# Copying projections out of PSUM at once, and handing a tile's attention outputs over behind the next tile's scores

## The chip, the core and the metric

The kernel runs on one core of a Trainium2 chip. The metric is the device time of the program in microseconds (us). TensorE (PE) multiplies and writes to PSUM; VectorE (DVE), ScalarE (ACT) and GpSimd (POOL) compute; SyncE (SP) only issues DMAs. ACT and POOL can issue DMAs as well. Each engine works through its own instructions in order.

## The reference, cut to what matters

One layer is computed for a prompt of 1024 tokens (tiles 0 to 7 of 128 rows) and for 8 x 16 new sample tokens (tile 8):

```python
n1 = rmsnorm(h); qa, ka, va, fl, qb, kb, vb, ga, gb = split(n1 @ w_in)
qa, ka, qb, kb = rmsnorm per head           # 8 heads x 64 in each of two mixers
log_f = log_sigmoid(fl + b_f); c = cumsum(log_f)
ya = softmax(qa @ ka.T / 8 + c_i - c_j, causal) @ va            # mixer A
yb = softmax(qb @ kb.T / 8 + relative bias, band of 9 chunks of 64) @ vb   # mixer B
# the sample tokens attend to 2048 (A) or 512 (B) cached rows per sequence as well
h += (sigmoid(ga) * (ya @ w_up_a) + sigmoid(gb) * (yb @ w_up_b)) @ w_out
h += PEER(rmsnorm(h))     # 8 heads pick 16 of 16384 experts: two top-16 and a gather
h += sigmoid(rmsnorm(h) @ w_ple_gate) * (p @ w_ple_proj)
```

k, v and log_f of the new tokens are outputs too. Weights and activations of the large products are split into a high and a low part, and a product is made of three matmuls.

## The kernel before, in words

The tiles are in two groups: group 0 is tiles 8, 0, 1, 2, group 1 is tiles 3 to 7. The phases of the span follow each other: norm and attention of group 0 (to about 500 us), its merge (gates and w_out), routing of group 0 (its remainder reaches into the next stretch), attention of group 1 (790 to 1391 us), its merge, routing of group 1 (to about 2010 us), `expand_phase` (2010 to 2256 us), `dense_phase` (to about 3870 us) and `ple_phase`. The experts of group 0 are fetched by 1024 gathers (`gather_steps`, POOL issues, DVE multiplies and adds), which are laid between the other work from the attention of group 1 on: 400 of them before `expand_phase`, the others in `dense_phase`. Matmuls `hd` of 36 blocks of experts (`hidden_phase`) fill PE in routing and expansion.

The attention of a group walks over eight units (`UNITS`; a unit is two heads of one mixer: 0 to 3 of A, 4 to 7 of B). For each unit, `project` makes a tile's projection `z` (k, q, v in 384 columns, 24 matmuls) in one of two PSUM banks of pool `z`, normalises k and q into `kq`, copies v into `vU`, transposes k and q through a bank `tp` and keeps them as `kT` and `qp`. Between the projections of a unit stand the attention steps of the unit before (`last`): `prompt` for prompt tiles, `decode` for tile 8. `prompt` makes, for each of the two heads, the scores `N` in a PSUM bank, the row minimum on DVE, `softmax_rows` (two passes of ACT and a reciprocal on DVE) into `p`, transposes of `p` into a bank `pt`, their copies `pT` (L80, called from `evac`), and the output matmuls `po` (L497), which use 64 of the 128 columns of the array: head 0 writes partitions 0 to 63 of `po`, head 1 partitions 64 to 127. The banks `tp`, `pt`, `po` share one pool, with three banks for group 0 and two for group 1. `decode` does the same against the cached rows `kcd` and `vcd`, which SP loads into a ring of `KC` buffers; its output matmuls `pod` (L591) use 32 columns each, for four sequences in turn.

The order within an engine is not written by hand. A scheduler walks over the program with a priority that follows the order of the code (shifted for some phases: gathers, routing and `hidden_phase` come later than their place) and a model of when buffers are free, and it fixes each engine's list; a buffer that is asked for while all of its pool are held must be waited for. SP's loads and stores are one such list.

## Time and profile before

| | us |
|---|---|
| median of 3 runs | 4042.02 |
| lowest and highest run | 4021.49, 4048.87 |
| the profiled execution | 4036.04 |
| its span in the profile | 4033.9 |
| PE busy in the span | 3674.5 (91%) |
| DVE busy | 2939.1 (73%) |
| POOL busy | 1865.5 (46%) |
| ACT busy | 1446.2 (36%) |

The span is the time from the first to the last instruction of the program in one execution; 2.1 us of the execution lie around it. A busy share is an average over phases with different limits, and a busy PE can still be a PE that is behind. PEld is PE's loading of weights, which can lie beside matmuls.

### The profile page before, as it was taken

Reading aid. Unit: us, or ns where it says so; the run is one execution under the profiler, and the core shown is the slowest. Engines: PE = TensorE matmul, PEld = TensorE weight load, DVE = VectorE, ACT = ScalarE, POOL = GpSimd, SP = SyncE. Lnnn points to the kernel's source line nnn. Section 1 sums busy time; section 2 is a strip of 40 time slices with the busy share of each in tenths; the row PEclk is TensorE's granted clock in tenths of the full one; section 3 lists DMA queues with packets and bytes.
Section 4 is the critical chain, followed back from the end, with each engine's and each line's share of the span. In section 5 each row is a group of like instructions: output and inputs, shape, how many; then the busy total and the mean of one; then the engine's idle time right before and its main releaser. Section 6 shows DMA issues by size and latency. Waiting matters only on the chain.

```text
span 4033.9 us, 57386 instructions
## 1 busy us (share of the span) xinstructions
PE 3674.5 (91%) x20520; PEld 3032.9 (75%) x20520; DVE 2939.1 (73%) x5531; ACT 1446.2 (36%) x3307; POOL 1865.5 (46%) x1440
## 2 busy tenths in 40 slices
PE   7998899868888798899898899999999999999989
PEld 6555567656676565699898888888888888888866
DVE  5122202899887776889998698888888888888862
ACT  5444422346555510223488422222222222222231
POOL 5111032127667655553276355555555555555510
PEclk9999999879999999899999999999999999999999
DMA  6777733328888888983345789988989898989942
GB/s 207 239 237 208 229 96 120 103 74 262 276 284 263 285 317 297 329 268 115 109 189 219 274 307 310 320 311 310 330 313 317 307 325 314 325 302 307 313 159 72
DMA packets 415118, 1002.50 MB, mean 249 GB/s; under 512 B 38816, under 2 KB 170352, under 8 KB 412400
## 3 DMA queue, kind: packets, MB, share of 16 engines
q0 software_dynamic: 147456, 536.94, 38.7%
q1 hardware_dynamic: 267376, 461.90, 34.4%
q8 instruction: 161, 2.64, 0.3%
q14 instruction: 125, 1.02, 0.1%
HBM read 917.19 MB, written 81.50 MB: 248 GB/s over the span
## 4 chain that ended last, share of the span: by engine, by line
PE 30%; DVE 19%; DMA 19%; issue 18%; POOL 12%; ACT 2%; SPq 0%; POOLq 0%; DVEq 0%; ACTq 0%
DMA v<-in_pv,gi 7%; POOL u L813 6%; DMA u<-in_pu,gi 6%; PE hd L964 5%; POOL v L813 3%; DVE gya L818 3%; DVE u L816 3%; PE pg L933 3%; PE Sd L547 2%; PE py L1015 2%; PE py L1017 2%; PE py L1016 2%; PE pu L638 1%; DMA vs<-in_pv 1%; PE z L209 1%
## 5 line engine op out<-in xcount | busy, mean ns | idle before, releaser
L813 POOL DMA_INDIRECT v<-in_pv,gi x512 | 680.3, 1329 | 582.8 <-DVE gya L818 451.2
L813 POOL DMA_INDIRECT u<-in_pu,gi x512 | 663.4, 1296 | 505.7 <-DVE u L816 374.8
L816 DVE SCALAR_TENSOR_TENSOR u<-u,gn 128x1024 f32<-128x1024 f32 x512 | 628.2, 1236 | 169.0 <-DMA u<-in_pu,gi 167.3
L818 DVE SCALAR_TENSOR_TENSOR gya<-v,hid,gya 128x1024 f32<-128x1024 f32 x512 | 661.3, 1292 | 120.0 <-DMA v<-in_pv,gi 115.5
L1015 PE MATMUL py<-vh,wh 128*128 128x512 f32 x1280 | 507.7, 398 | 44.2 <-ACT wh L946 23.6
L964 PE MATMUL hd<-aTh,uh 128*128 128x320 f32 x2048 | 485.1, 314 | 24.0 <-ACT gp L967 13.7
L1017 PE MATMUL py<-vh,wl 128*128 128x512 f32 x1280 | 498.3, 395 | 5.8 <-DVE wl L947 5.5
L1016 PE MATMUL py<-vl,wh 128*128 128x512 f32 x1280 | 502.8, 394 | 0.0
L964 PE MATMUL hd<-aTh,ul 128*128 128x320 f32 x2048 | 484.1, 314 | 5.5 <-DVE ul L947 4.2
L964 PE MATMUL hd<-aTl,uh 128*128 128x320 f32 x2048 | 484.1, 313 | 0.0
L964 PEld LDWEIGHTS hd<-aTh,uh 128*128 128x128 f32 x2048 | 351.9, 191 | 35.1 <-ACT gp L967 15.0
L964 PEld LDWEIGHTS hd<-aTh,ul 128*128 128x128 f32 x2048 | 349.6, 190 | 12.6 <-DVE ul L947 6.9
L964 PEld LDWEIGHTS hd<-aTl,uh 128*128 128x128 f32 x2048 | 351.3, 191 | 4.0
L1015 PEld LDWEIGHTS py<-vh,wh 128*128 128x128 f32 x1280 | 242.9, 190 | 102.3 <-ACT wh L946 29.7
L946 ACT CAST vh<-vs 128x1024 fp32r<-128x1024 f32 x128 | 134.0, 1052 | 483.3 <-DMA vs<-in_pv 241.9
L1017 PEld LDWEIGHTS py<-vh,wl 128*128 128x128 f32 x1280 | 243.2, 190 | 61.2 <-DVE wl L947 10.6
L1016 PEld LDWEIGHTS py<-vl,wh 128*128 128x128 f32 x1280 | 242.9, 190 | 46.9
L946 ACT CAST uh<-us 128x1024 fp32r<-128x1024 f32 x128 | 134.2, 1048 | 293.0 <-PE hd L964 285.3
L946 ACT CAST wh<-ge 128x640 fp32r<-128x640 f32 x128 | 91.9, 727 | 402.7 <-DVE ge L993 213.4
L1018 DVE TENSOR_TENSOR yacc<-yacc,py 128x1024 f32<-128x1024 f32 x160 | 192.5, 1215 | 15.0 <-PE py L1017 15.0
L497 PE MATMUL po<-pT,vU 128*64 128x128 f32 x1056 | 153.0, 290 | 34.6 <-ACT pT L80 34.0
L933 PE MATMUL pg<-obb,ga 128*128 128x128 f32 x1280 | 158.8, 279 | 26.5 <-POOL ga L924 19.5
(1051 smaller groups left out, 7361.0 us busy)
## 6 DMA issues: line engine op xcount, KB each, us to landing
us<-in_uT SPq DMA_DIRECT2D x128, 512.0 KB
vs<-in_pv SPq DMA_DIRECT2D x128, 512.0 KB
G_d<-stage SPq DMA_DIRECT2D x10, 4096.0 KB
gj<-G_d SPq DMA_DIRECT2D x64, 640.0 KB
kcd<-in_kA SPq DMA_DIRECT2D x128, 256.0 KB
vcd<-in_vA SPq DMA_DIRECT2D x128, 256.0 KB
ge_d<-gp SPq DMA_DIRECT2D x36, 320.0 KB
ge<-ge_d SPq DMA_DIRECT2D x36, 320.0 KB
```

The source lines that it names most:

```text
L497: nc.tensor.matmul(po[64 * h:64 * h + 64, 0:P], vU[:, k0 + j, 64 * h:64 * h + 64], pT[:, j, :], start=j == 0, stop=j == nk - 1)
L547: nc.tensor.matmul(ps[32 * b4:32 * b4 + 32, :], q3[:, 4 * s + b4, :], rhs, start=br == 1 and q < nch, stop=True)
L813: nc.gpsimd.indirect_dma_start(out=r, out_offset=None, in_=I["pu" if k < P else "pv"], in_offset=bass.IndirectOffsetOnAxis(ap=gi[:, kk:kk ...
L816: nc.vector.scalar_tensor_tensor(r, r, 1.0, n2, op0=OP.mult, op1=OP.mult, accum_out=hid[:, kk:kk + 1])
L818: nc.vector.scalar_tensor_tensor(ya, r, hid[:, kk:kk + 1], ya, op0=OP.mult, op1=OP.add)
L933: nc.tensor.matmul(pg[:, c * P:(c + 1) * P], ga[:, b0 + c, :], ob[:, b0 + c, :], start=True, stop=True)
L946: nc.scalar.copy(out_h, src)
L964: nc.tensor.matmul(ps[sp][:, 0:Nw], a[:, k, :], b[:, k, sp * Nw:(sp + 1) * Nw], start=k == 0 and q == 0, stop=k == 7 and q == 2)
L1015: nc.tensor.matmul(py[:, c], wh[:, ns], vh[:, c], start=a, stop=False)
L1016: nc.tensor.matmul(py[:, c], wh[:, ns], vl[:, c], start=False, stop=False)
L1017: nc.tensor.matmul(py[:, c], wl[:, ns], vh[:, c], start=False, stop=z)
L1018: nc.vector.tensor_tensor(yacc[n], yacc[n], py, op=OP.add)
```

## The change

The change has six parts; the first four lie in the attention.

- `project` copies k and q (256 columns) and v out of the bank `z` by two ACT copies at once; the squares, and the multiplication by the norm, then read the copy in SBUF. Before, the squares and DVE's multiplication read `z`, and v was copied last.
- `prompt` ends after the softmax of both heads and gives back a function `outputs`, which makes the transposes, the copies `pT` and the output matmuls. `order` puts a tile's `outputs` behind the next tile's scores (the last tile's at the end of its unit). The bank `po` is asked for after the transposes and no longer at the start.
- The output matmuls take the two heads in turn: block j of head 0, block j of head 1, block j + 1 of head 0.
- The stores of k, v, log_f, of `kT_d` and `v_d`, and further on those of `ge_d` (`hidden_phase`) and `G_d` (`expand_phase`), are issued by ACT and no longer by SP: 215 in all, 160 of them in `project`.
- Buffers: `KC` 17 for 15, three `p` for two, one `Dn` for two, `qp` of group 0 six for eight. `sel_p` holds 8 columns and is broadcast to 128 where it is read (its making is left out of the diff, as are lines that only take the new `PB`).
- `expand_phase` makes each one-hot tile `oa` by two DVE instructions of 128x512, where it was one of 128x1024.

```diff
-KC = 15
+KC = 17
...
-PB = (2, 2)
+PB = ((3, 2), (3, 2))
...
-    sel_p = const.tile([P, 8, P], F32R, name="sel_p")
+    sel_p = const.tile([P, 8], F32R, name="sel_p")
...
-                Dn = at.tile([P, 2, 256], F32, tag="Dn", name=f"Dn{g}{u}")
+                Dn = at.tile([P, 2, 256], F32, tag="Dn", name=f"Dn{g}{u}", bufs=1)
...
+            vt = vU[:, slot[t], :]
+            nc.scalar.copy(kq, z[:, 0:256])
+            nc.scalar.copy(vt, z[:, 256:384])
+            sq = at.tile([P, 64], F32, tag="sq", name=f"sq{nm}", bufs=2)
             for h in range(4):
-                nc.scalar.activation(kq[:, 64 * h:64 * h + 64], z[:, 64 * h:64 * h + 64], AF.Square, accum_out=ss[:, h:h + 1])
+                nc.scalar.activation(sq, kq[:, 64 * h:64 * h + 64], AF.Square, accum_out=ss[:, h:h + 1])
             r = rstd_of(ss[:, 0:4], 64, 4, f"kq{nm}")
-            nc.vector.tensor_tensor(kq.rearrange("p (h c) -> p h c", h=4), z[:, 0:256].rearrange("p (h c) -> p h c", h=4),
-                                    r.unsqueeze(2).broadcast_to([P, 4, 64]), op=OP.mult)
+            k4 = kq.rearrange("p (h c) -> p h c", h=4)
+            nc.vector.tensor_tensor(k4, k4, r.unsqueeze(2).broadcast_to([P, 4, 64]), op=OP.mult)
             nc.vector.tensor_tensor(kq[:, 0:P], kq[:, 0:P], kn[:, br, :], op=OP.mult)
-            vt = vU[:, slot[t], :]
-            nc.scalar.copy(vt, z[:, 256:384])
...
             if ko is not None:
-                nc.sync.dma_start(ko[rows, cu * P:(cu + 1) * P], kq[:, 0:P])
-                nc.sync.dma_start(vo[rows, cu * P:(cu + 1) * P], vt)
+                nc.scalar.dma_start(vo[rows, cu * P:(cu + 1) * P], vt)
...
-            qp = at.tile([P, 2, P], F32, tag="qp", name=f"qp{nm}", bufs=2 * nts if g == 0 else nts + 1)
+            qp = at.tile([P, 2, P], F32, tag="qp", name=f"qp{nm}", bufs=nts + 2 if g == 0 else nts + 1)
...
                 nc.scalar.copy(kTs, tp[:, 0:P])
+                nc.scalar.dma_start(ko[rows, cu * P:(cu + 1) * P], kq[:, 0:P])
...
+                if ko is not None:
+                    nc.scalar.dma_start(ko[rows, cu * P:(cu + 1) * P], kq[:, 0:P])
...
-                    nc.sync.dma_start(kT_d[u, :, t * P:(t + 1) * P], kT[:, t * P:(t + 1) * P])
-                    nc.sync.dma_start(v_d[u, :, t, :], vt)
-                pending.append([lambda: prompt(g, u, br, t, n, qp, kT, vU, Dn, at, yT)])
+                    nc.scalar.dma_start(kT_d[u, :, t * P:(t + 1) * P], kT[:, t * P:(t + 1) * P])
+                    nc.scalar.dma_start(v_d[u, :, t, :], vt)
+                tail = []
+                pending.append([lambda: tail.append(prompt(g, u, br, t, n, qp, kT, vU, Dn, at, yT)), lambda: tail[0]()])
...
-            if TS not in tiles:
-                return p
-            d = p[tiles.index(TS)]
-            r = [x for i, x in enumerate(p) if i != tiles.index(TS)]
-            out = [[d[0]], [r[0][0], d[1]], [r[1][0], d[2]], [r[2][0], d[3]]]
+            d = [[f] for f in p[tiles.index(TS)]] if TS in tiles else [[] for _ in p]
+            r = [x for i, x in enumerate(p) if tiles[i] != TS]
+            k = len(d) - len(r)
+            out = d
+            for i, (scores, outputs) in enumerate(r):
+                out[i + k] = [scores] + out[i + k]
+                out[min(i + k + 1, len(out) - 1)].append(outputs)
             return out
...
-        po = bank(f"po{nm}")
+        ps_ = []
...
-                    nc.tensor.matmul(N[:, c0:c1], sel_p[:, 2 * u + h, :], cP[:, c0:c1], start=False, stop=not last)
+                    nc.tensor.matmul(N[:, c0:c1], sel_p[:, 2 * u + h:2 * u + h + 1].broadcast_to([P, P]), cP[:, c0:c1], start=False, stop=not last)
...
-            p = softmax_rows(N[:, 0:W], W, m, at, f"{nm}{h}")
-            pT = at.tile([P, pmax[0] // P, P], F32, tag="pT", name=f"pT{nm}{h}", bufs=PB[pmax[0] > 512])
-            for j0 in range(0, nk, 4):
-                j1 = min(nk, j0 + 4)
-                ps = bank(f"pt{nm}{h}{j0}")
-                for j in range(j0, j1):
-                    nc.tensor.transpose(ps[:, (j - j0) * P:(j - j0 + 1) * P], p[:, j * P:(j + 1) * P], ident)
-                evac(pT[:, j0:j1, :], ps[:, 0:(j1 - j0) * P].rearrange("p (j c) -> p j c", c=P))
+            ps_.append(softmax_rows(N[:, 0:W], W, m, at, f"{nm}{h}"))
+
+        def outputs():
+            pTs = []
+            for h, p in enumerate(ps_):
+                pT = at.tile([P, pmax[0] // P, P], F32, tag="pT", name=f"pT{nm}{h}", bufs=PB[pmax[0] > 512][1])
+                for j0 in range(0, nk, 4):
+                    j1 = min(nk, j0 + 4)
+                    ps = bank(f"pt{nm}{h}{j0}")
+                    for j in range(j0, j1):
+                        nc.tensor.transpose(ps[:, (j - j0) * P:(j - j0 + 1) * P], p[:, j * P:(j + 1) * P], ident)
+                    evac(pT[:, j0:j1, :], ps[:, 0:(j1 - j0) * P].rearrange("p (j c) -> p j c", c=P))
+                pTs.append(pT)
+            po = bank(f"po{nm}")
             for j in range(nk):
-                nc.tensor.matmul(po[64 * h:64 * h + 64, 0:P], vU[:, k0 + j, 64 * h:64 * h + 64], pT[:, j, :],
-                                 start=j == 0, stop=j == nk - 1)
-        nc.scalar.copy(yT[:, u, n * P:(n + 1) * P], po[:, 0:P])
+                for h, pT in enumerate(pTs):
+                    r = slice(64 * h, 64 * h + 64)
+                    nc.tensor.matmul(po[r, 0:P], vU[:, k0 + j, r], pT[:, j, :], start=j == 0, stop=j == nk - 1)
+            nc.scalar.copy(yT[:, u, n * P:(n + 1) * P], po[:, 0:P])
+
+        return outputs
...
-                nc.vector.tensor_tensor(oa, iota_i.unsqueeze(1).broadcast_to([P, 2, P, 4]),
-                                        rb[:, 0, cw].rearrange("p (b c) -> p b c", b=2).unsqueeze(2).broadcast_to([P, 2, P, 4]),
-                                        op=OP.is_equal)
+                for b in range(2):
+                    nc.vector.tensor_tensor(oa[:, b, :, :], iota_i,
+                                            rb[:, 0, c0 + 4 * b:c0 + 4 * b + 4].unsqueeze(1).broadcast_to([P, P, 4]), op=OP.is_equal)
...
-                    nc.sync.dma_start(G_d[2 * n + c0 // 64], stage)
+                    nc.scalar.dma_start(G_d[2 * n + c0 // 64], stage)
...
-                nc.sync.dma_start(ge_d[q], ge)
+                nc.scalar.dma_start(ge_d[q], ge)
```

On PE, in the attention of group 1, at a tile with five blocks (the number behind a name counts tiles of the program). The kernel before: each head's transposes are followed by its own output matmuls.

```order
L494 MATMUL pt_12613<-ident,p_12607 128x128 x4
L494 MATMUL pt_12619<-ident,p_12607 128x128
L497 MATMUL po_12599<-pT_12612,vU_11582 64x128 x5
L494 MATMUL pt_12640<-ident,p_12634 128x128 x4
L468 MATMUL N_12735<-kT_12149,qp_12195 128x512
L469 MATMUL N_12735<-cP,sel_p 128x512
L471 LDWEIGHTS ident_b
L471 MATMUL N_12735<-m_diag,ident_b 128x128
L494 MATMUL pt_12646<-ident,p_12634 128x128
L497 MATMUL po_12599<-pT_12639,vU_11582 64x128 x5
```

The changed kernel: the transposes of both heads stand first, with the next tile's scores among them, and then the output matmuls of the two heads alternate (four of ten are shown).

```order
L503 MATMUL pt_12614<-ident,p_12491 128x128 x4
L503 MATMUL pt_12620<-ident,p_12491 128x128
L503 MATMUL pt_12624<-ident,p_12503 128x128 x4
L479 MATMUL N_12706<-kT_11688,qp_12126 128x512
L481 LDWEIGHTS ident_b
L481 MATMUL N_12706<-m_corner,ident_b 128x64
L479 MATMUL N_12706<-kT_11688,qp_12126 128x128
L503 MATMUL pt_12630<-ident,p_12503 128x128
L510 MATMUL po_12633<-pT_12613,vU_11689 64x128
L510 MATMUL po_12633<-pT_12623,vU_11689 64x128
L510 MATMUL po_12633<-pT_12613,vU_11689 64x128
L510 MATMUL po_12633<-pT_12623,vU_11689 64x128
```

What moved: ten output matmuls of one tile stand in one piece and alternate between `pT` of head 0 and of head 1, where they stood in two pieces of five.

On ACT, in the attention of group 1. The kernel before: the squares read `z`, and the copies `vU`, the last readers of two banks `z`, stand ten places later.

```order
L312 ACTIVATE kq_11170,ssz_11171<-z_11145 128x64 x4
L449 ACTIVATE p_11000<-p_11000,sm_11001 128x1024
L80 COPY pT_10971<-pt_10972 128x512
L80 COPY pT_10971<-pt_10978 128x512
L447 ACTIVATE p_11108,sm_11109<-N_11103,mn_11105 128x512
L449 ACTIVATE p_11108<-p_11108,sm_11109 128x512
L80 COPY pT_11005<-pt_11006 128x512
L80 COPY pT_11005<-pt_11012 128x512
L499 COPY yT_9030<-po_10957 128x128
L318 COPY vU_11052<-z_11055 128x128
L318 COPY vU_11052<-z_11145 128x128
```

The changed kernel: the two copies out of `z` stand together, the squares read `kq`, and two stores are issued by ACT.

```order
L454 ACTIVATE p_11922<-p_11922,sm_11923 128x768
L310 COPY kq_11997<-z_11972 128x256
L311 COPY vU_11689<-z_11972 128x128
L314 ACTIVATE sq_12001,ssz_11998<-kq_11997 128x64
L328 DMA out_vB<-vU_11689 128x128
L511 COPY yT_9087<-po_11855 128x128
L314 ACTIVATE sq_12001,ssz_11998<-kq_11997 128x64 x3
L347 DMA out_kB<-kq_11890 128x128
```

What moved: nothing behind the second copy reads `z`, and the stores stand in ACT's list.

## Rows read from the trace of the kernel before

**Rows 1.** Page's span; stretches: busy us of PE, PEld, DVE, ACT, POOL; clock, DMA share, GB/s.
```profile
span 4033.9 us, 57386 instructions
...
20.00:500.00 480.00, 421.54 (x3315) 279.53 (x3314) 132.74 (x361) 237.86 (x812) 110.72 (x135) 0.96 0.75 224
790.00:950.00 160.00, 116.16 (x531) 93.00 (x532) 158.16 (x783) 77.65 (x241) 70.97 (x62) 0.82 0.41 128
950.00:1391.00 441.00, 391.35 (x2263) 304.44 (x2263) 363.51 (x666) 262.36 (x742) 307.95 (x262) 0.97 0.84 273
1650.00:2010.00 360.00, 326.77 (x1965) 309.37 (x1964) 331.30 (x1317) 124.18 (x206) 152.36 (x98) 0.94 0.59 199
2010.00:2256.00 246.00, 216.59 (x1710) 210.90 (x1709) 212.29 (x166) 198.44 (x516) 161.13 (x88) 0.99 0.49 194
```

**Rows 2.** PE's waits, 20 to 500 us: who for whom, us in total, times, longest.
```profile
PE pod L591 <- DMA vcd<-in_vA: 25.6, 22, 2.4
PE z L209 <- ACT vU L318: 13.0, 3, 9.2
PE po L497 <- ACT pT L80: 7.6, 7, 1.4
```

**Rows 3.** PE's waits, 790 to 950 us.
```profile
PE z L209 <- ACT vU L318: 16.9, 4, 7.6
```

**Rows 4.** PE's waits, 950 to 1391 us.
```profile
PE po L497 <- ACT pT L80: 21.5, 20, 2.5
PE pt L494 <- ACT pT L80: 13.3, 12, 2.7
PE z L209 <- ACT vU L318: 9.6, 6, 4.4
```

**Rows 5.** L497 by stretch: PE and PEld busy us, clock, DMA share, GB/s.
```profile
20.00:500.00 480.00, 32.35 (x186) 20.52 (x186) 0.96 0.75 224
790.00:950.00 160.00, 14.09 (x87) 11.20 (x88) 0.82 0.41 128
950.00:1391.00 441.00, 104.91 (x773) 85.27 (x774) 0.97 0.84 273
```

**Rows 6.** Page's group of L497; one burst of it in the timeline.
```profile
L497 PE MATMUL po<-pT,vU 128*64 128x128 f32 x1056 | 153.0, 290 | 34.6 <-ACT pT L80 34.0
...
1254.74 1.31 PE L497 MATMUL po<-pT,vU 128*64 128x128 f32 x10
```

**Rows 7.** Timeline: one burst of decode's matmuls on four column groups, and weight loads.
```profile
229.73 2.46 PE L591 MATMUL pod<-vcd,pTd 128*32 128x128 f32 x81
...
229.15 2.77 PEld L591 LDWEIGHTS pod<-vcd,pTd 128*32 128x32 f32 x102 [0.34 <-ACT pTd L80]
```

**Rows 8.** SP queue's waits, 20 to 500 us.
```profile
SPq L328 <- DVE kq L316: 22.7, 10, 6.1
SPq L351 <- ACT vU L318: 16.5, 8, 4.3
...
SPq L350 <- ACT kT L345: 12.6, 12, 2.7
SPq L329 <- ACT vU L318: 12.4, 10, 1.9
```

**Rows 9.** DMA issues of L328 and L350: ns min/median/max, first and last start.
```profile
L328 SPq DMA_DIRECT2D out_kA<-kq x36: 332/344/1157, 63.7 to 1276.5; - x36
...
L350 SPq DMA_DIRECT2D kT_d<-kT x24: 319/345/1463, 43.8 to 465.9; - x24
```

**Rows 10.** ACT's copies by shape, 20 to 1391 us.
```profile
L318 ACT COPY vU<-z 128x128 f32<-128x128 f32 x72 | 18.0, 266 | 36.3 <-DVE kq L314 36.1
...
L80 ACT COPY pT<-pt 128x256 f32<-128x256 f32 x24 | 9.0, 373 | 15.6 <-PE pt L494 15.3
```

**Rows 11.** Page's group of L818, a gather's multiply-add.
```profile
L818 DVE SCALAR_TENSOR_TENSOR gya<-v,hid,gya 128x1024 f32<-128x1024 f32 x512 | 661.3, 1292 | 120.0 <-DMA v<-in_pv,gi 115.5
```

**Rows 12.** A group of 2010 to 2256 us, shapes kept apart.
```profile
L917 DVE TENSOR_TENSOR oa<-iota_i,rb 128x1024 bf16<-128x1024 bf16 x80 | 93.1, 1188 | 23.9 <-POOL ga L924 19.7 <-ACT rb L902 4.1
```

22 lines of the change are left out of this document (10 added, 12 removed).

## The prediction

> **What bounds the kernel now.** I read the stretches first, then PE's waits in each, then the queue of SP. PE is busy 3674 of 4034 us, so the first question is where the change touches PE's work or its gaps. It touches the two attention phases. In the first (20 to 500 us) PE is busy 421.5 of 480 us, ACT 237.9 and DVE 132.7: PE sets the pace [rows 1]. Its gaps there are waits for the cached values `vcd`, 25.6 us, for a bank `z`, 13.0, and for the copies `pT`, 7.6 [rows 2]. The second attention falls in two. Up to 950 us DVE is busy 158.2 of 160 us, with routing's remainder, and PE only 116.2 [rows 1]; PE's wait for `z` there, 16.9 us [rows 3], is a wait for DVE in disguise, since the copy that frees the bank stands behind DVE's multiplication. From 950 to 1391 us PE is busy 391.4 of 441 us and DVE 363.5, with gathers among its work [rows 1]; PE waits 21.5 us for `pT` before output matmuls, 13.3 before transposes, 9.6 for `z` [rows 4]. Behind the attention, routing from 1650 to 2010 us belongs to DVE (331.3 of 360 us), and in expansion PE (216.6 of 246), DVE (212.3) and ACT (198.4) are close together [rows 1]. In the dense phase nothing is edited.
>
> **Output matmuls of two heads in turn.** This is the largest term, and it is PE work and not a wait. One matmul of the program is two instructions in the trace, so 1056 instructions of L497 stand for 528. A burst of ten takes 1.31 us and one instruction 0.290 [rows 6]: (1.31 - 0.29) / 9 = 0.113 us from one to the next, all on the same 64 columns. The nearest row for work on other columns is `decode`, which takes four groups of 32 columns in turn: 81 instructions in 2.46 us [rows 7], so (2.46 - 0.28) / 80 = 0.027 us each, 0.109 for a round of four. A round takes about as long as one instruction of the burst above, so the groups run beside each other. Two groups should give 0.11 / 2 = 0.055 us each, 0.058 less than now. There are 186 instructions in the first attention and 773 in the second behind 950 us [rows 5]: 959 x 0.058 = 55.6 us; the 87 in the stretch that DVE bounds are not counted. Since PE is busy 88% of these two stretches, I take 50. Bounds: 0, if the two halves do not run together, and 1056 x 0.058 = 61.
>
> Here a rule speaks against the row. The Trainium skill, page "TensorE: Matmul & The Clock Gate", Part 3, says that a weight load overlaps with matmuls in flight only when its row group differs; these matmuls all use 128 rows, and by that rule the turn would gain nothing and the sum below would be 4009. The trace disagrees for 32 columns: 102 weight loads in 2.77 us [rows 7] are 0.027 us apart. No row shows it for 64 columns.
>
> **Projections copied at once.** The bank `z` is free after two ACT copies instead of after squares, POOL, DVE and a copy. The waits for it are 13.0, 16.9 and 9.6 us [rows 2 to 4]. Of the first and the last I count two thirds, 15, because the two copies themselves still have to come round on ACT; of the 16.9 under a full DVE I count 5. Together 20, between 0 and 39.5. What is late next is the transposes of k and q, which still need POOL and DVE; they have no reader until the next unit.
>
> **Outputs behind the next tile's scores.** PE's waits for `pT` are 7.6, 21.5 and 13.3 us, 42.4 in the stretches that PE bounds [rows 2, 4]. Two edits meet them: other matmuls stand between the softmax and its transposes, and the bank `po` is no longer held while the transposes run, so in the second attention `pt` has both banks of its pool instead of one. Against that, both `pT` of a tile are needed before its outputs, and three `p` buffers mean that the second head of the next tile waits until the first head's transposes are done. I count half, 21, between 0 and 42.
>
> **Stores moved from SP to ACT.** In the first attention SP waits 22.7 + 16.5 + 12.6 + 12.4 = 64.2 us in front of stores that are not ready [rows 8], and the loads of cached rows queue behind these. With the stores gone, and two more buffers in the ring, I count half of PE's wait for `vcd`, 12 of 25.6 us [rows 2]; the other half I leave to the DMA engines, whose share is already 0.75 [rows 1].
>
> The cost is ACT's. It gets 72 copies of 256 columns at 0.373 us (the same shape from PSUM, [rows 10]), 27 us, and 160 issues of stores at 0.344 us (SP's median, [rows 9]), 54 us: 81 us in stretches where it is busy 577.9 of 1081 us [rows 1]. ACT is not the bound, but its passes stand between PE's scores and outputs. What hides the 81 us is the 503 us in which ACT is idle; I put 10 on the path, between 0 and 81. No row shows a DMA issued by ACT. If it meets the same jams as SP in the first attention (1.157 us at worst for k, 1.463 for `kT_d`, [rows 9]), its 88 stores there cost up to 88 x 0.81 = 72 us more.
>
> **Gathers that move.** In the lists of the two kernels 194 gathers stand before the last projection of group 1 in the one before, 185 in the changed one; at the last split of w_out it is 341 and 328. So 13 gathers move into routing, at 1.292 us each [rows 11], 17 us of DVE work where DVE has 28.7 us left of 360 [rows 1]. I count 10, between 0 and 17.
>
> **Expansion.** Eighty instructions `oa`, 93.1 us in that stretch [rows 12], become 160 of half the size; at equal throughput nothing changes, and the first half can be read sooner. DVE idles 19.7 us there for POOL to give a buffer back [rows 12]. The ten stores `G_d` cost ACT 3.4 us of 47.6 us idle. I count 0, between -15 and +15. The smaller `sel_p`, the single `Dn` (units of B have a unit of A between them) and the smaller `qp` ring count 0: the first saves a few setup instructions, and a wait for the others would be on SP or ACT ahead of need.
>
> **The sum.** Gains 50 + 20 + 21 + 12 = 103, losses 10 + 10 = 20: 83 us off the profiled execution, 4036 - 83 = 3953. That execution is 6 us under the median of the runs before, so the median after should be **3959 us**.
>
> **The rivals.** *Absorbed gains* (14%): the engines wait for each other in order, and a faster PE only reaches the next wait for DVE or ACT sooner. For it speaks that DVE is at 82% from 950 us on, with gathers at fixed places in its list between the row minima; against it, that all of PE's waits for `pT` and `z` end on ACT, which is 59% busy there. Then only the `vcd` waits and part of `z`, 32 us, come through, less 20: 4024, median 4030.
>
> *The halves do not overlap* (8%): the rule above holds for 64 columns, and 50 us are missing: 4003, median 4009. Against it stands `decode` [rows 7].
>
> *ACT becomes the bound* (12%), the slower side: the issues on ACT jam as SP's do, and the softmax, the copies `pT` and the stores share one list. ACT's extra time is then 81 + 72 = 153 us. While under 93 us of it lies on the path the kernel still gains (103 less 10 for the gathers); with all of it there, 4036 - 93 + 153 = 4096, median 4102. For it speaks that in the first attention ACT would be busy some 350 of 450 us; against it, that a median issue takes 0.344 us.
>
> **How the numbers follow.** My forecast has 66%. 1% (40 us) is about what a measurement of this kernel can tell from no change, since the three runs before differ by 0.7%. Faster by over 1% means under 4002: the forecast, and a quarter of the second rival, 68%. Within 1%: the first rival and the rest of the second, 20%. Slower: the third, 12%. The low end takes the full terms: 61 + 39.5 + 42.4 + 25.6 = 168.5 off, and half of the losses, 10, put back, with the median's 6: 3884, so 3885. The high end, 4050, takes in the first two rivals and an ACT cost of half its worst, and leaves out most of the third.
>
> **What the changed profile would show.** The output matmuls: some 60 to 70 us busy in all instead of 153, and about 0.055 us from one to the next. Waits of PE for `vU` before a projection gone, and none of like size for `kq` in their place; waits of PE for `pT` halved; waits for `vcd` halved. DMA issues on ACT of about 0.34 us. The first attention shorter by about 30 us, the second by about 60, and routing longer by 10. I am wrong if the output matmuls stay 0.11 us apart, if ACT's issues take over 1 us, or if PE's waits keep their sum and only change their names; wrong the other way if the clock, 0.82 from 790 to 950 us [rows 1], is granted in full there because PE waits less.

## The result, and the profile after

The changed kernel takes 4011.19 us (median of 12 runs, 3999.80 to 4022.79) where the kernel before takes 4036.95 (12 runs beside it): a ratio of 0.9941, 95% interval 0.9928 to 0.9955. It is 26 us faster where the sum had 83, and 52 us above the forecast of 3959. The clock granted over the span is 0.961. The changed kernel's stretches, cut at the same events as those of before [rows 1] (columns as there), but for routing, which is cut here at the last w_out:

```profile
20.00:474.00 454.00, 394.11 (x3342) 275.63 (x3341) 134.73 (x364) 253.61 (x847) 110.93 (x133) 0.94 0.79 237
...
767.00:927.00 160.00, 112.78 (x542) 87.01 (x542) 157.74 (x773) 82.67 (x256) 70.12 (x59) 0.82 0.40 121
927.00:1347.00 420.00, 357.15 (x2257) 269.85 (x2255) 351.04 (x661) 272.09 (x768) 286.57 (x252) 0.96 0.83 273
...
1637.00:1982.00 345.00, 304.91 (x1899) 293.63 (x1898) 325.03 (x1296) 120.40 (x199) 158.09 (x95) 0.94 0.59 197
1982.00:2231.00 249.00, 213.90 (x1647) 205.00 (x1645) 220.99 (x251) 193.74 (x513) 145.64 (x88) 0.99 0.47 188
```

The row of [rows 1] for routing begins 36 us ahead of the last w_out. Cut there as well, the kernel before has:

```profile
1686.00:2010.00 324.00, 290.77 (x1806) 280.32 (x1805) 303.02 (x1273) 116.88 (x195) 131.00 (x81) 0.93 0.55 183
```

The stages, from the first or last instruction of PE on a named tile (start of group 0's gates, first projection of group 1, start of group 1's gates, last w_out, first and last matmul of the expansion, last `py`):

| us | before | after | difference |
|---|---|---|---|
| first attention (and norm) | 504.7 | 478.6 | -26.1 |
| second attention | 602.5 | 581.1 | -21.4 |
| its merge | 292.8 | 288.5 | -4.3 |
| routing of group 1 | 337.9 | 358.7 | +20.8 |
| expansion | 232.9 | 235.5 | +2.6 |
| dense phase | 1617.6 | 1623.5 | +5.9 |

The rest (first merge, tail) adds 4; the sum is the span's difference, 18. So the first attention came out as forecast (-30), the second gave a third of the 60, and routing cost twice the 10.

PE's waits from 20 to 474 us, beside [rows 2]:

```profile
PE ptd L590 <- ACT pTd L80: 16.4, 8, 4.8
PE pod L605 <- ACT pTd L80: 7.7, 7, 2.9
PE ydd L610 <- ACT obd L608: 4.5, 6, 1.6
PE pod L605 <- DMA vcd<-in_vA: 4.2, 5, 2.1
...
PE po L510 <- ACT pT L80: 3.4, 3, 1.2
```

The wait for `vcd` fell from 25.6 to 4.2 and the one for `z` behind `vU` is gone, but a wait of 16.4 for ACT stands before the decode's transposes `ptd`, where it was 0.7. So PE's idle time did not fall: it was 480 - 421.5 = 58 us and is 454 - 394.1 = 60. What fell is PE's busy time, by 27 us, and 22 of them lie in matmuls that the change does not edit, the decode's scores `Sd` (the same two stretches):

```profile
L547 PE MATMUL Sd<-kcd,qp 128*32 128x512 f32 x320 | 100.5, 615 | 1.8 <-DVE Nd L557 1.2 <-DMA kcd<-in_kA 0.6
...
L561 PE MATMUL Sd<-kcd,qp 128*32 128x512 f32 x320 | 78.8, 623 | 1.6 <-DMA kcd<-in_kA 1.1 <-ACT p L452 0.4
```

One instruction takes as long as before (615 and 623 ns), so more of them run beside each other. Each works on 32 columns; four sequences on four groups of columns, two instructions each, make a round of eight. Two pieces of PE's timeline in the kernel before:

```profile
125.72 1.05 PE L547 MATMUL Sd<-kcd,qp 128*32 128x512 f32 x2
...
130.92 1.06 PE L547 MATMUL Sd<-kcd,qp 128*32 128x512 f32 x8
```

A whole round takes no longer than one group by itself, so time is lost where other matmuls stand between the groups. In the kernel before, PE's timeline has 91 pieces of `Sd`, 43 of them of two instructions and 13 of eight; in the changed one it has 66, 11 and 19. With the hand-over undone `Sd` is busy 91.4 us (e8) and 97.4 (e15, against 83.6 in e14), so it is the hand-over that leaves more rounds whole. How the scheduler comes from it to this order is not shown.

From 767 to 927 us, beside [rows 3]:

```profile
PE tp L330 <- DVE kq L318: 15.0, 6, 3.5
...
PE z L207 <- ACT vU L311: 4.8, 2, 2.6
```

The wait for `z` is 4.8 instead of 16.9, and 15.0 appear for the same DVE one step later, at the transposes of k and q: under a full DVE the wait changed its name. The granted clock stays at 0.82 there. From 927 to 1347 us, beside [rows 4]:

```profile
PE pt L503 <- ACT pT L80: 15.6, 17, 3.1
PE po L510 <- ACT pT L80: 11.8, 13, 2.1
PE N L479 <- ACT p L452: 9.0, 9, 2.8
PE N L473 <- ACT p L452: 5.7, 8, 1.8
```

The wait for `pT` before output matmuls is about half, that before transposes is 15.6 instead of 13.3, that for `z` behind `vU` is gone, and scores `N` now wait 14.7 us for a softmax to free their bank.

The output matmuls by stretch, beside [rows 5], and one burst of the timeline, beside [rows 6]:

```profile
20.00:474.00 454.00, 24.76 (x173) 13.51 (x174) 0.94 0.79 237
767.00:927.00 160.00, 8.03 (x96) 6.18 (x96) 0.82 0.40 121
927.00:1347.00 420.00, 57.64 (x768) 46.38 (x768) 0.96 0.83 273
...
1250.62 1.31 PE L510 MATMUL po<-pT,vU 128*64 128x128 f32 x18
```

Eighteen instructions now take the 1.31 us that ten took. 24.76 + 8.03 + 57.64 = 90 us against 151 in [rows 5], and PE is busy 3615.1 us in the span instead of 3674.5. The two halves of 64 columns do run beside each other. The Trainium skill, page "TensorE: Matmul & The Clock Gate", Part 3, has weight loads overlap with matmuls in flight only where the row group differs. All rows are used here, and the trace disagrees: eighteen weight loads of L510, 0.137 us each (median), would fill 2.5 us if they stood one behind the other.

DMA issues on ACT (ns min/median/max), beside [rows 9]; none of the 215 took over 0.77 us:

```profile
L328 ACTq DMA_DIRECT2D out_vA<-vU x36: 338/344/768, 54.3 to 1226.8; - x36
...
L352 ACTq DMA_DIRECT2D kT_d<-kT x24: 326/332/549, 42.2 to 442.4; - x24
```

The gathers' DVE work in routing (1637 to 1982 us), beside [rows 11], and the halved one-hot tiles, beside [rows 12]:

```profile
L830 DVE SCALAR_TENSOR_TENSOR u<-u,gn 128x1024 f32<-128x1024 f32 x45 | 64.1, 1425 | 10.8 <-DMA u<-in_pu,gi 10.6
L832 DVE SCALAR_TENSOR_TENSOR gya<-v,hid,gya 128x1024 f32<-128x1024 f32 x16 | 26.5, 1657 | 0.0
...
L932 DVE TENSOR_TENSOR oa<-iota_i,rb 128x512 bf16<-128x512 bf16 x160 | 95.9, 656 | 17.5 <-POOL ga L938 13.2 <-ACT rb L916 4.2
```

61 gathers are worked off in routing; before it was 47 (31 and 16).

**Where the 60 us went.** The second attention whole, before and after, and in each the two largest waits of DVE:

```profile
791.00:1393.00 602.00, 507.37 (x2795) 397.70 (x2794) 522.51 (x1442) 340.16 (x985) 380.22 (x324) 0.93 0.73 235
...
DVE gya L818 <- DMA v<-in_pv,gi: 30.8, 34, 1.8
DVE u L816 <- DMA u<-in_pu,gi: 30.8, 36, 2.1
```

```profile
768.00:1349.00 581.00, 469.41 (x2797) 356.60 (x2796) 509.08 (x1428) 355.41 (x1025) 357.01 (x311) 0.92 0.71 232
...
DVE u L830 <- DMA u<-in_pu,gi: 28.5, 34, 3.4
DVE gya L832 <- DMA v<-in_pv,gi: 23.2, 27, 2.5
```

PE's busy time fell by 38 us, the stage by 21. DVE's busy time and its waits for gathered rows make 522.5 + 61.6 = 584 of 602 us before and 509.1 + 51.7 = 561 of 581 after: in both it is DVE's list that fills the stage. 224 gathers were worked off there, now 211. PE's clock is no rival for the missing 40 us: it was granted at 0.93 and is at 0.92, which makes some 84 and 93 us at 1.2 GHz (an estimate from the two rows above), and 9 us more at half speed cost at most 5 us.

### The profile page after: what moved, and what is told of

It is laid out like the page before. It is cut to its first block, busy times and chain, and to the rows that moved or that the text cites. A ratio compares the mean times of both kernels' runs of the same rounds, so it can differ in the third digit from the quotient of the medians.

```text
span 4015.7 us, 57411 instructions
## 1 busy us (share of the span) xinstructions
PE 3615.1 (90%) x20520; PEld 2991.5 (74%) x20520; DVE 2957.5 (74%) x5610; ACT 1475.3 (37%) x3379; POOL 1868.6 (47%) x1436
## 4 chain that ended last, share of the span: by engine, by line
DVE 23%; DMA 21%; PE 21%; issue 20%; POOL 13%; ACT 3%; POOLq 0%; SPq 0%; ACTq 0%; DVEq 0%
DMA v<-in_pv,gi 9%; POOL u L827 6%; DMA u<-in_pu,gi 6%; POOL v L827 5%; DVE gya L832 3%; DVE u L830 3%; PE pg L947 2%; DMA vs<-in_pv 2%; PE Sd L561 2%; PE pu L652 1%; PE hd L978 1%; POOL ga L938 1%; DVE topi L743 1%; DVE sc L744 1%; DVE topi L746 1%
## 5 line engine op out<-in xcount | busy, mean ns | idle before, releaser
L827 POOL DMA_INDIRECT u<-in_pu,gi x512 | 675.3, 1319 | 498.0 <-DVE u L830 370.4
L978 PEld LDWEIGHTS hd<-aTh,uh 128*128 128x128 f32 x2048 | 350.7, 190 | 25.6 <-ACT gp L981 14.5
L947 PEld LDWEIGHTS pg<-obb,ga 128*128 128x128 f32 x1280 | 153.9, 193 | 42.9 <-POOL ga L938 21.0
```

The costliest lines, as they stand in the source:

```text
L827: nc.gpsimd.indirect_dma_start(out=r, out_offset=None, in_=I["pu" if k < P else "pv"], in_offset=bass.IndirectOffsetOnAxis(ap=gi[:, kk:kk ...
L947: nc.tensor.matmul(pg[:, c * P:(c + 1) * P], ga[:, b0 + c, :], ob[:, b0 + c, :], start=True, stop=True)
L978: nc.tensor.matmul(ps[sp][:, 0:Nw], a[:, k, :], b[:, k, sp * Nw:(sp + 1) * Nw], start=k == 0 and q == 0, stop=k == 7 and q == 2)
```

## The experiments

**Theory A**: the gathers in DVE's list set the pace of the second attention, so the change brings there what the scheduler moved out of it, and pays for that in routing. **B**: ACT's added copies and issues. **C**: new waits on the few `p` and `pT`. The stage times below are cut as in the table above; "gathers" are those worked off in the stage. Each row is one profiled execution. In the changed kernel and in e4 DVE works off the same list up to routing, and their second attentions differ by 7 us: a difference of that size in that stage tells nothing.

| kernel | first attention | second attention | gathers in it | DVE busy in it | routing (gathers in it) |
|---|---|---|---|---|---|
| before | 504.7 | 602.5 | 224 | 523 | 337.9 (47) |
| after | 478.6 | 581.1 | 211 | 509 | 358.7 (61) |
| e3_no_turn | 476.3 | 606.6 | 223 | 522 | 341.0 (50) |
| e4_g0_386 | 479.7 | 588.0 | 211 | 510 | 341.7 (47) |
| e7_stores_sp | 464.1 | 562.5 | 206 | 498 | 362.9 (65) |
| e8_no_defer | 483.7 | 549.0 | 201 | 491 | 375.9 (73) |
| e6_nogather_before | 507.6 | 559.5 | 0 | 267 | 270.7 (0) |
| e5_nogather_after | 478.2 | 514.8 | 0 | 269 | 270.0 (0) |
| e11_short_dve | 479.2 | 532.8 | 222 | 331 | 294.1 (51) |
| e12_small_rows | 479.7 | 535.5 | 206 | 500 | 337.4 (52) |
| e2_before_ring5 | 503.9 | 588.0 | 236 | 534 | 311.2 (32) |
| e1_ring5 | 478.5 | 734.0 | 324 | 644 | 270.8 (0) |
| e10_before_even_ring5 | 507.2 | 579.9 | 220 | 517 | 270.1 (0) |
| e9_even_ring5 | 475.6 | 628.3 | 222 | 528 | 265.0 (0) |
| e13_ring5_fits | 479.3 | 573.5 | 226 | 522 | 332.2 (44) |
| e14_fits_sp | 467.7 | 567.4 | 225 | 516 | 326.3 (42) |
| e15_fits_sp_no_defer | 482.9 | 569.1 | 219 | 512 | 342.5 (49) |
| e16_fits_sp_even | 463.8 | 569.9 | 225 | 518 | 308.5 (31) |
| e17_best_no_turn | 474.6 | 572.2 | 224 | 520 | 318.7 (34) |
| e18_best_no_copies | 463.4 | 571.5 | 229 | 528 | 309.0 (28) |

**A larger ring, in either kernel** (e2 with the small `sel_p` as well, which makes room).

```diff
-RING = 4
+RING = 5
```

> The changed kernel with five gather buffers instead of four. Theory A: from 927 us to the end of the second merge the gathers in DVE's list set the pace, about 2.2 us each with four buffers (191 in 420 us, 128 in 290 us in the changed kernel). With five buffers the pace should be 2.2 x 4/5 = 1.76 us. The scheduler puts 288 of them before the last projection instead of 185, and all 400 before the last split of w_out, so the second attention should get longer by about 40 us (288 gathers), the second merge shorter by about 35, and routing, which loses its 61 gathers, shorter by about 80: about 3940 us in all. Theory B (ACT's added 81 us pace the second attention): attention does not get longer, since ACT's work is the same, and the pace of gathers does not matter: the total moves only by routing's share. Theory C (new waits from few p and pT buffers): as B.

> The kernel before with five gather buffers; to make room it takes the smaller sel_p from the change, nothing else. The scheduler puts 205 gathers before the last projection (194 before) and 356 before the last split of w_out (341). Theory A: at 1.76 us each the second attention (602 us before) gets shorter until PE's work bounds it, by 20 to 40 us, the second merge by about 20, routing by about 20 (44 gathers for 59): about 3970 us. Theories B and C say that gathers do not pace it: within 10 us of before.

e1: 3987.49 us, ratio 0.9882 [0.9859, 0.9904]. e2: 3906.63 us, 0.9692 [0.9667, 0.9717]: the kernel before gained 128 us and passed the changed one. 78 of these lie in the dense phase (1617.6 to 1539.3), the rest in the second attention, its merge and routing. e1 gained nearly as much in the dense phase (1548.6) and lost it in the second attention, 734 us. Neither theory had expected that; it is taken up below.

**The turn undone.**

```diff
-            for j in range(nk):
-                for h, pT in enumerate(pTs):
+            for h, pT in enumerate(pTs):
+                for j in range(nk):
```

> The changed kernel, with the output matmuls of head 0 before those of head 1. PE's busy time should go up by about 59 us again (the 0.11 us step). The scheduler puts 195 gathers before the last projection (185 in the changed kernel, 194 before). Theory A: the second attention is as long as its gathers, about 20 us longer than in the changed kernel, and routing about 15 us shorter: total within 15 us of the changed kernel, about 4015 us, with PE's gaps in the second attention smaller by the 45 us that PE works more. If PE paced it, the second attention would be 45 us longer and the total about 4060.

4013.87 us, 0.9949 [0.9934, 0.9964], as the changed kernel. Its second attention has 223 gathers and 606.6 us, its routing 50 and 341.0: of the 25 us that it lost in one stage it got back 18 in the other, and 13 in the expansion and the dense phase.

**Fewer gathers ahead of the expansion.**

```diff
-G0 = 400
+G0 = 386
```

> The changed kernel with 386 gathers called for ahead of the dense phase instead of 400; the dense phase, which has room for 640, takes the 14. Their places before the last projection (185) and before the last split of w_out (328) do not change, so all 14 leave routing. Theory A: routing, which DVE bounds, gets shorter by 14 x 1.3 to 1.6 us, 18 to 22 us, and the total is about 3992 us. If routing is longer for another reason than the gathers moved into it, it keeps its 345 us and the total stays at 4011.

4002.44 us, 0.9916 [0.9893, 0.9938]. Routing lost 14 gathers and 17 us (341.7 for 358.7); the second attention kept its 211. (The profiled execution of e4, 4021.03 us, is the slowest of its five.) Over the kernels with four buffers, routing is 270 us without gathers and 1.42 to 1.53 us longer for each one in it.

**No gathers ahead of the dense phase**, in the changed kernel and in the one before.

```diff
-G0 = 400
+G0 = 0
```

> The changed kernel with no gather ahead of the dense phase; 640 run in it and 384 behind it, so the total is much longer (by some 700 us) and only the stages are read. Theory A: without gathers the second attention is bound by PE and ACT, and the changed kernel's is shorter than that of the kernel before (next run) by most of what PE lost in work, 40 to 60 us, instead of the 21 us seen with gathers. Theory B: ACT's added work is still there, so the difference stays near 20 us. Theory C: the waits for p and pT stay, the difference stays near 20 us.

> The kernel before with no gather ahead of the dense phase, to be compared with the run above. Theory A: its second attention, 602 us with gathers, falls to some 540 us, where PE's work (about 507 us in those stretches) bounds it, and PE's wait for vU before a projection stays. Theories B and C say nothing about this run; what counts is the difference to the run above.

4602.68 and 4664.88 us in one run each; the gathers all come later. The second attention of the two, in the columns of [rows 1]:

```profile
767.00:1282.00 515.00, 453.10 (x2797) 353.20 (x2796) 269.30 (x1082) 352.57 (x1022) 88.57 (x100) 0.94 0.16 48
```

```profile
795.00:1354.00 559.00, 495.29 (x2795) 390.28 (x2795) 266.62 (x1089) 338.40 (x981) 89.86 (x100) 0.94 0.15 44
```

With DVE at 269 and 267 us, PE's 42 us less work shorten the stage by 45. ACT's added work and the new waits are in e5 too, so neither B nor C takes the gain away by itself. The six kernels of the table with four buffers and whole gathers take 2.69 to 2.79 us of the second attention per gather in it, whatever their PE does.

**The stores back on SP.** The five calls of `project` that store k, v, `kT_d` and `v_d`, like this one:

```diff
-                nc.scalar.dma_start(vo[rows, cu * P:(cu + 1) * P], vt)
+                nc.sync.dma_start(vo[rows, cu * P:(cu + 1) * P], vt)
```

> The changed kernel with the 160 stores of project issued by SP again (those of log_f, ge_d and G_d stay on ACT). Theory B: ACT loses 54 us of issues, and the second attention gets shorter by 15 us or more at the same number of gathers; the first attention gets longer, since SP waits before stores again and PE waits for vcd more, by about 10 us. Theory A: the second attention goes by its gathers (179 for 185 before the last projection), about 10 us shorter, and routing gets as much longer: total within 10 us of the changed kernel, but for the first attention.

3994.10 us, 0.9893 [0.9865, 0.9921]: 17 us under the changed kernel. In the profiled execution (3976.75 us, the fastest of four) the first attention is 14.5 us shorter. The second is 18.6 shorter with five gathers less, at 2.73 us per gather, as theory A has it.

**The outputs behind their own scores.**

```diff
-                out[i + k] = [scores] + out[i + k]
-                out[min(i + k + 1, len(out) - 1)].append(outputs)
+                out[i + k] = [scores, outputs] + out[i + k]
```

> The changed kernel, with a tile's outputs called for right behind its own scores instead of behind the next tile's. Theory C: the waits of PE for p before scores (14.7 us from 927 us on) go away and the second attention gets shorter. Theory A: the second attention goes by its gathers (180 for 185), about 10 us shorter, routing as much longer (72 for 72 + 5), total within 10 us. If the delay itself brought something, PE's waits for pT before output matmuls rise from 11.8 us again to 20 or more and the total by 10 to 20 us.

3997.66 us, 0.9908 [0.9876, 0.9940]. The first attention is 5 us longer, with 12.6 us more of `Sd` and a wait for `pT` before output matmuls of 18.0 us (3.4 in the changed kernel), against a wait for `pTd` before `ptd` of 1.7 (16.4); the second has ten gathers less and is 32 us shorter, routing has twelve more and is 17 us longer. With gathers moving this much, the run says nothing of the hand-over itself there.

**Gathers held to the units, five buffers** (e9 from the changed kernel; e10 from the one before, the same edits and the small `sel_p`; the rest of G0 is held behind the last `sm` of the second attention).

```diff
-RING = 4
+RING = 5
+GU = 8 * (27,)
-G0 = 400
+G0 = 336
-G2 = 5
+G2 = 6
...
-            nc.vector.tensor_tensor(kq[:, 0:P], kq[:, 0:P], kn[:, br, :], op=OP.mult)
+            at_z = nc.vector.tensor_tensor(kq[:, 0:P], kq[:, 0:P], kn[:, br, :], op=OP.mult)
+            if g == 1 and n == 0:
+                gathers(GU[UNITS.index(u)], at_z)
```

> The changed kernel with five gather buffers, 27 gathers held behind the first projection of each unit, 222 in the second attention by the order, 114 in merge, none in routing, 688 left to dense (G2 = 6). Theory A (gathers in DVE's list pace the second attention, the merge and the dense phase): in the runs so far the second attention took 2.69 to 2.79 us per gather in it with four buffers, and 515 us with none. With five buffers it was 2.27 at best, so 222 x 2.27 = 504 no longer pace it: second attention about 530, merge 255, routing 270, dense about 1560; 3800 in all. Rival B (ACT's added copies and issues, or the new waits on pT, hold the second attention): it stays at 570 or more although the gathers have room, 3850 or above.

> The kernel before with the same five buffers, the small sel_p and the same gathers held to the units (220 in the second attention by the order). Theory A: its second attention falls to its length without gathers, 560 us, or a little above, since PE and not the gathers sets the pace; 3860 in all, so that the change is worth 60 us on this ground (24 in the first attention, 35 to 45 in the second) where it was worth 26. Rival: the change's gain in the second attention stays at 20 or less whatever the gathers do, and the two kernels are 45 us apart or less.

3983.14 us, 0.9885 [0.9860, 0.9909], and 3952.13 us, 0.9805 [0.9784, 0.9826]. Both are late for a reason of mine: 688 gathers are too many for the dense phase, and the last end 89 and 85 us behind its last matmul. Theory A's numbers failed all the same: 628 us in the second attention of e9, where 530 was expected, 580 in that of e10, where it was 560 or a little above, and the changed kernel slower than the one before. PE stands in one wait of 93 us there, for `z`; in e1 it is one of 184 us. PE's wait in e1, and ACT's timeline at its end:

```profile
PE z L207 <- ACT vU L311: 187.7, 5, 184.0
...
905.98 1.04 ACT L797 COPY oh<-ab 128x1024 bf16<-128x1024 bf16 x1 [21.79 <-DVE ij L804]
907.31 1.04 ACT L797 COPY oh<-ab 128x1024 bf16<-128x1024 bf16 x1 [0.28 <-DVE ij L804]
927.35 1.04 ACT L797 COPY oh<-ab 128x1024 bf16<-128x1024 bf16 x1 [18.99 <-DVE ij L804]
929.61 1.04 ACT L797 COPY oh<-ab 128x1024 bf16<-128x1024 bf16 x1 [1.22 <-DVE ij L804]
950.76 1.04 ACT L797 COPY oh<-ab 128x1024 bf16<-128x1024 bf16 x1 [20.11 <-DVE ij L804]
952.13 1.04 ACT L797 COPY oh<-ab 128x1024 bf16<-128x1024 bf16 x1 [0.33 <-DVE ij L804]
977.85 0.37 ACT L310 COPY kq<-z 128x256 f32<-128x256 f32 x1 [24.67 <-DVE fl L306]
```

All sixteen copies `oh` of routing's remainder stand in ACT's list ahead of the first copy out of `z` in group 1, and they wait for DVE, some 20 us for every pair; PE has filled both banks and stands. In the changed kernel with four buffers, no `oh` stands ahead of the first four projections' copies. The layout of SBUF tells why. In group 1 the third buffer `p`, which the change adds, ends at byte 132,672 of a partition. Routing's `iota16`, which every `oh` is compared with, begins at 136,128 with four gather buffers and at 132,032 with five. So that buffer is free only when routing is through. How the scheduler came from there to this order I can't show step by step; e13 tests the cause.

**Five buffers without that overlap, and the parts of the change on this ground.** e13 takes one `qp` of group 1 away (1 KB); e14 is e13 with the stores on SP; e15 is e14 with the outputs behind their own scores; e16 is e14 with G0 = 390 and 29 gathers held per unit; e17 is e16 with the turn undone; e18 is e16 with the projections read in PSUM as before. The edits of e14, e15 and e17 are those of e7, e8 and e3; e13's, e16's and e18's:

```diff
-            qp = at.tile([P, 2, P], F32, tag="qp", name=f"qp{nm}", bufs=nts + 2 if g == 0 else nts + 1)
+            qp = at.tile([P, 2, P], F32, tag="qp", name=f"qp{nm}", bufs=nts + 2 if g == 0 else nts)
```

```diff
+GU = 8 * (29,)
-G0 = 400
+G0 = 390
```

```diff
-            nc.scalar.copy(kq, z[:, 0:256])
-            nc.scalar.copy(vt, z[:, 256:384])
...
-                nc.scalar.activation(sq, kq[:, 64 * h:64 * h + 64], AF.Square, accum_out=ss[:, h:h + 1])
+                nc.scalar.activation(kq[:, 64 * h:64 * h + 64], z[:, 64 * h:64 * h + 64], AF.Square, accum_out=ss[:, h:h + 1])
...
+            nc.scalar.copy(vt, z[:, 256:384])
```

> The changed kernel with five gather buffers and one buffer qp less in group 1 (1 KB), so that the third buffer p of the second attention no longer lies on routing's iota16, as it does by 0.6 KB in e1 and e9, where PE stood 184 and 93 us in one wait for z behind ACT. 227 gathers in the second attention by the order, 117 in merge, 56 in routing. If that overlap was what spoiled e1 and e9, and the gathers' ring is what took the gain of the second attention: no single wait over 20 us, second attention 535 to 560, routing about 343, dense 1540; 3835 to 3875 in all, some 50 us under e2, the kernel before with the same ring. Rival: the overlap isn't the cause, or the change has little to give in the second attention: 3880 or above.

> As e13, and project's stores back on SP. In e7 that made the first attention 14 us shorter and left the second at the same time per gather. If the stores' issues on ACT cost the first attention what they save SP: 12 to 15 us under e13, all of it ahead of 480 us. If e7's gain was placement of gathers alone: within 5 us of e13.

> As e14, and a tile's outputs right behind its own scores, as in the kernel before. 220 gathers in the second attention by the order, 62 in routing. If the hand-over behind the next tile's scores is worth the 21 us of the prediction: 15 us or more over e14, in both attention phases. If the waits only move (e8 had 5 us more in the first attention): within 8 us of e14, less the 8 us that six more gathers cost in routing.

> As e14, with gathers(390) instead of 400 ahead of the expansion, the first 232 held behind the units' first projections (the order has 227 in the second attention as in e14): ten gathers leave routing for the dense phase. At 1.45 us each in routing: 13 us off; the dense phase had 24 us of room behind its last gather in e2, so it pays 0 to 10. 3810 to 3845.

> As e16, with each head's output matmuls in a row instead of two heads in turn. If PE's saved work (some 55 to 60 us busy in the two attention phases) reaches the end where the ring has five buffers: 25 us or more over e16. If DVE's list, its own 269 us and 1.1 us per gather, sets the second attention (91% busy in e13 to e16) and the first attention has PE waiting anyway: within 10 us of e16, PE's busy time in the second attention some 35 us higher and its idle time as much lower.

> As e16, with the projection read in PSUM as in the kernel before (squares and DVE's multiplication on z, then the copy of v). If the copies are worth the 20 us of the prediction: 15 to 25 over e16, 10 to 15 of it in the first attention, PE's wait for z back at 10 to 15 us there. If they are what is left of the first attention's gain (40 us with the stores on SP, 15 of it the hand-over): 25 in the first attention alone. If the 27 us of ACT copies cost what the bank saves: within 8 us of e16.

| kernel | median us | ratio to before, 95% |
|---|---|---|
| e13_ring5_fits | 3877.84 | 0.9604 [0.9574, 0.9634] |
| e14_fits_sp | 3855.45 | 0.9551 [0.9521, 0.9581] |
| e15_fits_sp_no_defer | 3893.24 | 0.9653 [0.9619, 0.9687] |
| e16_fits_sp_even | 3847.58 | 0.9537 [0.9506, 0.9567] |
| e17_best_no_turn | 3854.82 | 0.9549 [0.9521, 0.9576] |
| e18_best_no_copies | 3848.21 | 0.9529 [0.9506, 0.9553] |

e13 is 110 us under e1, its second attention is 573.5 us instead of 734, and its `oh` stand behind the first four projections again: the overlap was the cause, as far as one edit can tell (no run takes the `qp` away where nothing overlaps). That time is above the 535 to 560 expected, and the total above the 3835 to 3875. It is 14.5 under e2's with ten gathers less, and DVE is busy 522 of it: with five buffers, DVE's list still sets the stage, more by its own work and less by waiting (27 us for gathered rows, where it was 52). e13 is 29 us under e2: the first attention's 25, and little else.

e14 is 22 us under e13, 11.6 of it in the first attention, the rest in the second and in routing, 6 each. PE's waits there (20 to 463 us) are the old ones again:

```profile
PE pod L605 <- DMA vcd<-in_vA: 15.7, 22, 2.2
PE ydd L610 <- ACT obd L608: 6.4, 6, 3.0
```

The `vcd` wait is back, the wait for `pTd` before `ptd` is 2.2 us where e13 has 9.7, and that exchange is a gain. e15 is 38 us over e14: 15 in the first attention (13.8 of them busy time of `Sd`), 2 in the second, 16 in routing with seven more gathers, 8 in the expansion. e16 against e14: 18 us off routing for eleven gathers less, of which the expansion and the dense phase take 9.5 back. It missed the 3810 to 3845 expected; with e18 it is the fastest kernel here that computes everything, 4.6% under the one before. e17 is 11 us slower in the first attention, and PE is busy 17 us more in the second, which is 2 us longer; its total can't be told apart from e16's. The 35 us of busy time that were expected in the second are 17 beside a granted clock of 0.94, where e16 has 0.91. e18 is e16 to within a microsecond: PE waits 8.4 us for `z` in the first attention, and ACT is 18 us less busy there.

**What in a gather costs: DVE's pass or the transfer** (both from the changed kernel, four buffers).

```diff
-nc.vector.scalar_tensor_tensor(r, r, 1.0, n2, op0=OP.mult, op1=OP.mult, accum_out=hid[:, kk:kk + 1])
+nc.vector.scalar_tensor_tensor(r[:, 0:P], r[:, 0:P], 1.0, n2[:, 0:P], op0=OP.mult, op1=OP.mult, accum_out=hid[:, kk:kk + 1])
```

> The changed kernel; DVE's two gather operations work on the first 128 of 1024 columns only, the gathers themselves move all (the sums over the other columns are left out). 223 gathers stand in the second attention by the order, 114 in merge, 63 in routing. If the transfer and the ring of four buffers set the pace: second attention still 2.4 to 2.7 us per gather, 540 to 600 us, merge at 2.2 per gather, 250 us. If DVE's own 1.2 us per gather set it: second attention 515 to 530, as without gathers. Routing falls to about 275 either way, since it is DVE's work that counts there.

```diff
-r = gat.tile([P, D], F32, tag="ring", name=f"{'uv'[k // P]}{t}_{k % P}", bufs=RING)
+r = gat.tile([P, 256], F32, tag="ring", name=f"{'uv'[k // P]}{t}_{k % P}", bufs=RING)
```

> The changed kernel; each gather moves rows of 256 instead of 1024 columns (a quarter of the bytes, other rows of the table), DVE works on 1024 columns as before by reading them four times (the sums are other sums). 207 gathers stand in the second attention by the order. If transfer and ring set the pace: second attention 520 to 540, merge 250, and the dense phase, also paced by gathers, near its PE work of 1540 to 1560. If DVE's time sets the pace: second attention about 570 and merge about 285 as in the changed kernel.

3804.52 and 3821.05 us in one run each. The second attention and DVE's first wait in e11:

```profile
766.00:1299.00 533.00, 461.15 (x2797) 356.45 (x2796) 330.83 (x1444) 356.56 (x1025) 310.17 (x321) 0.93 0.76 263
...
DVE u L830 <- DMA u<-in_pu,gi: 75.5, 66, 4.0
```

and in e12:

```profile
769.00:1305.00 536.00, 454.08 (x2799) 351.50 (x2797) 500.62 (x1426) 357.43 (x1026) 367.87 (x306) 0.94 0.32 94
...
DVE junk L833 <- DMA u<-in_pu,gi: 2.2, 3, 1.3
```

Either half taken away gives 533 to 536 us in the second attention, 269 and 257 in the merge (288.5 in the changed kernel) and 1532 and 1526 in the dense phase (1623.5). Routing of e11 is 294 us, where about 275 was expected. Neither rival of that pair held alone: DVE waits more when its pass is short and is busy 500 us when nothing makes it wait. What fills the stage is the sum, 269 us of attention, some 1.14 us of passes per gather ((509 - 269) / 211), and the waits between. So theory A stands in this form: the gathers set the second attention by what they take in DVE's list. B holds for the first attention alone (e7, e14), and C for none of the runs.

## Why the prediction was wrong

The forecast, 3959, was 52 us too low. The range held the time; the sign was right, and the size was "within 1%", which had 0.20.

**Output matmuls in turn, 50 us: the step that failed.** The price per instruction was right: 61 us less busy time in the three stretches, against 56 to 61 worked out. (By that price 153 us become 92, and 92.8 were measured over the whole span; the "60 to 70 us busy in all" of the prediction does not follow from its own term.) Wrong was "since PE is busy 88% of these two stretches, I take 50". In the second attention PE's busy share was no sign that it set the pace: DVE's 363.5 us in [rows 1] were read as 82%, and its waits for gathered rows, 61.6 us over the stage, were not read at all, though [rows 11] has 115.5 us of them over the span. Undoing the turn moved the total by 3 us with four buffers (e3) and by 7, not distinguishable, with five (e17); the first attention got 2 us shorter by it in e3 and 11 longer in e17. Without early gathers the second attention gains 45 us from all parts together (e5, e6), so the 60 would have been near only there.

**Projections copied at once, 20 us.** The waits for `z` did go. On the path the edit is worth nothing that e18 can tell (0.9529 against 0.9537).

**Outputs behind the next scores, 21 us.** The mechanism was wrong as well. Of the 42.4 us of waits for `pT`, 3.4 + 11.8 + 15.6 = 30.8 are left, and 14.7 us of waits of `N` came in their place. The edit is worth 5 us (e8) and 15 us (e15) in the first attention, where what it brings is above all something that the prediction does not have: rounds of `Sd` left whole, 12.6 and 13.8 us less busy time. In the second it is 2 us between e14 and e15. What it does to the placement of gathers is as large as that.

**Stores on ACT, 12 gained and 10 paid.** The gain was larger than I took (21 of the 25.6 us of `vcd`), and the cost larger still: the first attention is 14.5 us (e7) and 11.6 us (e14 against e13) shorter without the move. An issue takes 0.34 us as estimated (160 of them are 55 us, not 54) and there are no jams; what was mis-sized is the share of ACT's time that lies on the path, since PE waits for ACT's `pTd` in the decode.

**The first attention, 30 us in all: 26.** The total came out by errors that cancel. With the stores on SP it is 40 us shorter than before (e16); the turn is worth 11 of them, the hand-over 15, the copies 0. The prediction looked for the 30 us mostly in waits that end; PE's idle time stayed and its work ran in less time, most of it in `Sd`. The remaining 14 I did not take apart; PE's wait for `vcd` is 17.2 us in e16 against 25.6, and the larger ring `KC` and the smaller constants are left.

**Gathers that move, 10 us.** By the lists 13; in the trace 14 more in routing, at 1.45 us each (358.7 - 270.0 = 88.7 us for 61), so 20 of the 20.8 measured. The stage has no slack for them: I took part of DVE's 28.7 idle us as free, and cut at the last w_out it was 21.

**Absorbed gains**, at 14% and 4030 us, names what happened in the second attention, DVE's list with gathers at fixed places; I set it against PE's waits ending on ACT, and ACT's own longest wait there ended on DVE (54.9 us for `sm` from 950 to 1391 us, before). It was too pessimistic for the first attention. ACT as the bound and halves that do not overlap are both refuted.

## What to carry to other kernels

Before a saving on one engine is counted, add to every other engine's busy time its waits for data that only it uses: where the sum fills the stage, as DVE's 522 + 62 of 602 us here, the saving stays in the stage only as far as that sum shrinks. Work that a scheduler may place anywhere needs a price per stage (2.7 us per gather in the attention, 1.45 in routing), and each edit has to be compared at equal placement. An edit that moves nothing but order can change the price of work that it doesn't touch: a round of `Sd` on four groups of columns took as long as one group (1.06 and 1.05 us), so it pays to look whether the rounds stand together. When a buffer is added, look at what its neighbours now overlap in SBUF: 0.6 KB cost 110 us (e1 against e13).

## What was unexpected of the hardware

A gather's two DVE passes are slower on average in routing than in the attention: 1425 and 1657 ns against 1220 and 1281 ns for the same shapes in the same run. That is the work of a few long passes. In the changed kernel 8 of all 1024 passes take over 1.5 us, all of them in routing, and each lies beside POOL's subtraction `ul`; the others in routing take 1.21 and 1.26 us. One pair:

```profile
1801.46 2.40 POOL L961 TENSOR_TENSOR ul<-us,uh 128x1024 fp32r<-128x1024 f32 x1
...
1801.58 3.36 DVE L832 SCALAR_TENSOR_TENSOR gya<-v,hid,gya 128x1024 f32<-128x1024 f32 x1
```

Of the ten passes that overlap an `ul`, eight are long (1.9 to 4.1 us); none of the 37 beside POOL's small powers for `kq` (128x4) or the 22 beside its memsets is. In the kernel before there are again eight long passes, all beside a POOL subtraction of this kind. So the length of a gather's pass goes with what POOL does at that moment. No run takes the subtraction away, so that POOL makes DVE wait is not shown beyond this.
